# Second-layer conditioning formed by VectorE inside the first MLP, weight sums moved from GpSimd to VectorE, attentions in a new order: a two-layer hybrid diffusion step on one Trainium2 core

## The chip, the cores and the metric

The kernel runs on one core of a Trainium2 chip. The metric is device time in microseconds for one execution; runs are compared by their median. The core has a matrix engine (TensorE; PE in the profile, with the loads of its stationary operand shown as PEld), a vector engine (VectorE, DVE), a scalar engine (ScalarE, ACT), GpSimd (POOL) and SyncE (SP), which here issues every DMA. Matrices live in on-chip SBUF; TensorE writes into PSUM, of which there are eight banks, and VectorE and ScalarE read from there.

## The reference, cut to what matters

Two trunk layers (`DEPTH = 2`) run over 128 context tokens and 512 latent tokens, 640 in all, 1024 wide, in float32. Each layer is modulated by six vectors that come from one conditioning vector per token group:

```python
sh1, sc1, g1, sh2, sc2, g2 = jnp.split(jax.nn.silu(cvec) @ lw['w_ada'] + lw['b_ada'], 6, axis=-1)
h = rmsnorm(x, lw['norm1_g']) * (1 + sc1) + sh1
...
x = x + g1 * (mix @ lw['w_out'])
h2 = rmsnorm(x, lw['norm2_g']) * (1 + sc2) + sh2
x = x + g2 * (jnp.square(jax.nn.relu(h2 @ lw['w_up'])) @ lw['w_down'])
```

`w_ada` is 1024 x 6144 for each layer, and there are only two different vectors `cvec` (context and latent), so the conditioning of a layer is a product of a 1024 x 6144 matrix with two columns. Nothing in it depends on the tokens; it has to be there before the layer uses it: `sh1` and `sc1` (sections 0 and 1 below) at the layer's first normalisation, `g1` (section 2) at the output projection, sections 3, 4 and 5 in the MLP.

## The kernel before, in words

**Precision.** Every large product is formed from float32 values split into a rounded high part (type fp32r) and the rest: high x high, high x low, low x high. So a weight tile (`wr`, raw, 512 KB, 128 x 1024) is loaded by SP, copied into a high tile `wh` by ScalarE (L401 or L416), and the difference `wl` is formed by VectorE (L409, the helper `sub`). TensorE then does three matmuls for each piece.

**Stages.** After the input (to 48 us) each layer has a projection, the attentions, a second normalisation, and the MLP. Projection and attentions are planned by a list scheduler in the kernel's Python (class `Plan`): each piece of work is a task with an estimated cost, a priority and its operands, and the plan's order becomes the program's order for each engine. The order of the attention's parts is written by hand as a string of tokens (`"seq"` in `KP`, L64): `s0`, `s1` the windowed heads, `D0`, `d0`, `D1`, `d1` the differential heads with their preparation, `V0`, `M0`, `m0`, `M1`, `m1` the latent heads, `w0` to `w2` the output projections, and `c1` one conditioning of 256 columns.

**Conditioning before the change.** `conditioning` (L552) forms 256 columns of one section: two loads of 512 KB, sixteen matmuls of TensorE (L578, tile `pa`), a ScalarE copy, two transposes (L583), and two or three small VectorE operations that add the bias and, for sections 1 and 4, form the multiplier `amul`. Layer 0's first two sections are formed in the beginning, from wider loads. Its other sections, 2, 3, 4 and 5, and sections 1 and 0 of layer 1 are formed during layer 0's attentions (24 conditionings); sections 2, 4, 3 and 5 of layer 1 during layer 1's attentions (16).

**The MLP** isn't planned by `Plan` but written out as a loop (from L1745 on). The hidden width of 4096 is cut into eight groups of 512. A group's up-projection is two pairs of 128-wide tiles; each pair is done by seven products instead of eight (a Strassen-Winograd form over two halves of the model width and two halves of the tokens). The seven are called `A11 A12 S2 S3 S1 A22 S4`. One such product is a block: 12 matmuls of 320 columns (L1871). An up half of a group is therefore 14 blocks. A group's down-projection is eight blocks of 24 matmuls (L544 to L546). The order is: down 0, up 1, then up g+1 and down g in turn; down 7 is done in the next plan.

Seven products need sums. Those of the tokens are formed by VectorE during the first eight blocks (`wino_tokens`, tiles `Tl`, `Th`). Those of the weights are formed from the two raw tiles `r0` and `r1` of a pair by four GpSimd operations of 128 x 512: two early ones in `advance` (L1784) as soon as the second raw tile's load has been written into the program (`r1` low half, and `ws`), two late ones in `pool_late` (L1778) after the tile `A12` has been prepared (`r0` low half = S1's weights, `r0` high half = S4's).

Results: blocks A11, S2 and S1, S4 add into one PSUM bank X one after another, S3 and A22 into a bank Z, A12 into Y:

```python
z = {"A11": "X", "A12": "Y", "S2": "X", "S3": "Z", "S1": "X", "A22": "Z", "S4": "X"}[q]
new = q in ("A11", "A12", "S3")
```

After A11, S2 and S3 ScalarE copies the bank out (`pe`). After A12, S1 and A22 VectorE adds bank and copy (L1886) and squares the positive part (L1887); after S4 ScalarE takes the positive part (L1881) and VectorE squares it (L1882). One block later each result is split into the high and low part of `Gt` (ScalarE L401, VectorE L409). After a down block VectorE adds the product, times g2, to the residual `xT` (L747).

For each block the program's order is: its matmuls; the operations on its result; the split of the block before; two steps of the token sums; then `prep` (L1804), which prepares weight tiles. There are four `wh` and four `wl` buffers, so the tile prepared after a block is the one three tiles ahead, just when the block was the last user of a buffer. `prep` calls `advance`, which writes the loads into the program: four raw buffers, and the load of raw tile n is written once tile n-4 has been used. Each engine does its instructions in the program's order; SP issues a load when a raw buffer is free.

## Time and profile before

| | |
|---|---|
| runs | 1782.9, 1694.25, 1690.71 us (median 1694.25) |
| the profiled execution | 1687.62 us, of which the span from the first to the last instruction is 1685.8 us; mean granted TensorE clock 0.99 |

By stage, from the busy time by stretches:

| stretch, us | stage | us | PE busy | DVE busy | ACT busy | POOL busy |
|---|---|---|---|---|---|---|
| 0 to 48 | input, first conditioning | 48 | 32.05 | 30.28 | 23.53 | 0.20 |
| 48 to 160 | projection, layer 0 | 112 | 109.59 | 78.00 | 43.63 | 0.00 |
| 410 to 455 | second normalisation, first up-projection | 45 | 39.01 | 33.54 | 25.81 | 2.61 |
| 455 to 828 | MLP, layer 0 | 373 | 369.00 | 265.28 | 134.07 | 79.91 |
| 828 to 870 | last down-projection, normalisation | 42 | 41.33 | 34.06 | 22.18 | 0.00 |
| 870 to 984 | projection, layer 1 | 114 | 110.48 | 75.46 | 41.31 | 0.00 |
| 1228 to 1270 | second normalisation, first up-projection | 42 | 36.27 | 32.36 | 25.39 | 2.59 |
| 1270 to 1643 | MLP, layer 1 | 373 | 369.52 | 264.49 | 134.30 | 81.46 |
| 1643 to 1686 | last down-projection, output | 43 | 31.52 | 28.34 | 8.32 | 0.00 |

The attentions, 160 to 410 and 984 to 1228, are shown with the prediction.

How to read the profile's lines. A line of a stretch gives its bounds and length, then for each engine the busy microseconds and the number of instructions (x), the granted TensorE clock, the share of DMA in use and GB/s. A line of the timeline gives start, duration, engine, the line of the kernel, the operation, output <- inputs with shapes, and in brackets how long the engine stood idle before and what ended that. Durations overlap: an engine can begin an instruction a little before the last one has ended, so what one costs in a row of them is read from start to start. A line of waits gives who waited for whom, microseconds in total, how often, and the longest.

### The profile page before, as it was taken

What the parts mean: (1) busy time and instruction counts of PE and PEld (TensorE: products, weight loads), DVE (VectorE), ACT (ScalarE), POOL (GpSimd) and SP (SyncE); (2) the same over time, 40 slices, a digit from 0 to 9 for tenths busy, and PEclk for the clock granted to TensorE, in tenths of its full rate; (3) what the DMA queues carried; (4) which work ended last, traced back from release to release, by engine and by line L of the source; (5) the groups of instructions that cost most, each with busy time, mean ns of one, the idle gap of its engine ahead of it and who ended that gap; (6) DMA issues with size and microseconds to landing.
All of it is one profiled execution on the core that took longest, in us unless ns stands there. A gap on an engine that the chain in (4) does not pass through costs nothing.

```text
span 1685.8 us, 29293 instructions
## 1 busy us (share of the span) xinstructions
PE 1609.4 (95%) x11035; PEld 1443.1 (86%) x11035; DVE 1270.1 (75%) x3315; ACT 792.7 (47%) x1773; POOL 204.0 (12%) x164
## 2 busy tenths in 40 slices
PE   6999999898999999999999999999989999999997
PEld 4787678577999999999988766866889999999997
DVE  5875889877788666776586769999888866766666
ACT  4533776774544332333264346776463523343231
POOL 0000012000133122220000000300002322212200
PEclk9999999999999999999999999999999999999999
DMA  9433453532113212232223234124021212221121
GB/s 328 131 92 112 144 178 95 166 105 88 51 51 101 88 57 83 76 101 95 65 66 99 82 113 156 53 91 147 26 77 62 91 60 88 89 100 65 62 76 63
DMA packets 67388, 163.20 MB, mean 97 GB/s; under 512 B 6896, under 2 KB 31280, under 8 KB 67248
## 3 DMA queue, kind: packets, MB, share of 16 engines
q1 hardware_dynamic: 67248, 161.34, 29.5%
q8 instruction: 87, 1.43, 0.3%
q14 instruction: 53, 0.43, 0.1%
HBM read 153.15 MB, written 8.16 MB: 96 GB/s over the span
## 4 chain that ended last, share of the span: by engine, by line
PE 76%; DVE 14%; ACT 3%; DMA 2%; issue 2%; POOL 0%; DVEq 0%; SPq 0%; ACTq 0%; POOLq 0%
PE pu L1871 19%; PE pu L544 8%; PE pu L545 8%; PE pu L546 8%; PE po L544 3%; PE pt L1108 3%; PE O L1122 3%; PE po L546 3%; PE po L545 3%; PE pz L842 3%; PE pz L844 3%; PE pz L843 3%; DVE wl L409 2%; PE pu L1484 2%; PE pa L578 1%
## 5 line engine op out<-in xcount | busy, mean ns | idle before, releaser
L409 DVE TENSOR_TENSOR wl<-wr,wh 128x512 fp32r<-128x512 f32 (+2 forms) x290 | 289.3, 1018 | 68.0 <-ACT wh L401 34.2
L401 ACT ACTIVATE wh<-wr 128x512 fp32r<-128x512 f32 (+1 forms) x228 | 161.0, 736 | 272.1 <-PE pu L545 154.4
L544 PE MATMUL pu<-Gt,wh 128*128 128x384 f32 (+1 forms) x896 | 276.6, 309 | 1.2 <-DVE r L1469 1.2
L546 PE MATMUL pu<-Gt,wl 128*128 128x384 f32 (+1 forms) x896 | 276.5, 309 | 0.0
L545 PE MATMUL pu<-Gt,wh 128*128 128x384 f32 (+1 forms) x896 | 276.5, 309 | 0.0
L747 DVE SCALAR_TENSOR_TENSOR xT<-pu,ada,xT 128x128 f32<-128x128 f32 x336 | 133.0, 432 | 122.0 <-PE pu L546 121.7
L544 PEld LDWEIGHTS pu<-Gt,wh 128*128 128x128 f32 x896 | 169.8, 190 | 1.6 <-DVE r L1469 1.6
L545 PEld LDWEIGHTS pu<-Gt,wh 128*128 128x128 f32 x896 | 169.9, 190 | 0.0
L546 PEld LDWEIGHTS pu<-Gt,wl 128*128 128x128 f32 x896 | 169.8, 189 | 0.0
L1871 PE MATMUL pu<-Tl,wh 128*128 128x320 f32 x448 | 138.1, 308 | 0.0
L1871 PE MATMUL pu<-Th,wl 128*128 128x320 f32 x448 | 138.1, 308 | 0.0
L1871 PE MATMUL pu<-Th,wh 128*128 128x320 f32 x448 | 138.1, 308 | 0.0
L842 PE MATMUL pz<-wh,hh 128*128 128x512 f32 (+1 forms) x320 | 127.0, 397 | 3.8 <-DVE m L775 1.1
L844 PE MATMUL pz<-wh,hl 128*128 128x512 f32 (+1 forms) x320 | 122.4, 382 | 0.1
L843 PE MATMUL pz<-wl,hh 128*128 128x512 f32 (+1 forms) x320 | 121.8, 381 | 0.6 <-DVE wl L409 0.6
L1060 DVE TENSOR_REDUCE stt<-sps 128x1 f32<-128x640 f32 (+2 forms) x160 | 116.4, 736 | 7.3 <-PE sps L1053 4.2
L1871 PE MATMUL pu<-hh,wh 128*128 128x320 f32 x336 | 104.9, 312 | 7.5 <-DVE r L1886 7.5
L1068 ACT ACTIVATE quad<-sps,stt 128x640 f32<-128x640 f32 (+2 forms) x128 | 91.2, 713 | 41.1 <-DVE stt L1060 40.4
L1871 PE MATMUL pu<-hh,wl 128*128 128x320 f32 x336 | 104.3, 311 | 0.0
L1871 PE MATMUL pu<-hl,wh 128*128 128x320 f32 x336 | 104.2, 310 | 0.0
L1447 POOL TENSOR_TENSOR xT<-xT,tm 128x256 f32<-128x256 f32 (+1 forms) x32 | 33.1, 1038 | 574.2 <-ACT tm L1443 570.0
L409 POOL TENSOR_TENSOR wr<-wr 128x512 f32<-128x512 f32 x28 | 40.3, 1441 | 467.6 <-DMA wr<-in_w_up 313.2
(311 smaller groups left out, 3884.8 us busy)
## 6 DMA issues: line engine op xcount, KB each, us to landing
wr<-in_w_ada SPq DMA_DIRECT2D x80, 512.0 KB, 4.1
wr<-in_w_up SPq DMA_DIRECT2D x64, 512.0 KB, 3.3
wr<-in_w_down SPq DMA_DIRECT2D x64, 512.0 KB, 3.5
wr<-in_w_in SPq DMA_DIRECT2D x24, 512.0 KB, 3.6
wr<-in_w_out SPq DMA_DIRECT2D x16, 512.0 KB, 3.8
wq<-in_w_ada SPq DMA_DIRECT2D x6, 1024.0 KB, 11.9
wr<-in_w_in SPq DMA_DIRECT2D x8, 416.0 KB, 3.6
xT<-in_xT SPq DMA_DIRECT2D x4, 640.0 KB, 6.6
```

The source lines that it names most:

```text
L401: S.activation(out=out, in_=in_, func=AF.Copy)
L409: eng.tensor_tensor(out=out, in0=a, in1=b, op=ALU.subtract)
L544: T.matmul(out=out, lhsT=w[0], rhs=a[0], start=first, stop=False)
L545: T.matmul(out=out, lhsT=w[0], rhs=a[1], start=False, stop=False)
L546: T.matmul(out=out, lhsT=w[1], rhs=a[0], start=False, stop=last)
L747: V.scalar_tensor_tensor(out=xT[:, m, a:b], in0=po[:, a - a0:b - a0], scalar=ada[l][:, sec, m, s:s + 1], in1=xT[:, m, a:b], op0=ALU.mult, ...
L842: T.matmul(out=out, lhsT=h_at(h, "h", k, tk), rhs=wh[:, x], start=(k == 0), stop=False)
L843: T.matmul(out=out, lhsT=h_at(h, "h", k, tk), rhs=wl[:, x], start=False, stop=False)
L844: T.matmul(out=out, lhsT=h_at(h, "l", k, tk), rhs=wh[:, x], start=False, stop=(k == KD - 1))
L1060: add("V", tV(we) - 0.01, lambda st=st, j=j, view=view: V.tensor_reduce(out=st.t[:, j:j + 1], in_=view(), axis=AX.X if kind == "sw" else A ...
L1068: S.activation(out=out, in_=view(), func=AF.Exp, bias=st.t[:, j:j + 1], accum_out=st.t[:, 4 + j:5 + j])
L1871: T.matmul(out=out, lhsT=w_[:, k], rhs=a_[:, k], start=new and k == 0 and y == 0, stop=k == 3 and y == 2, skip_group_check=True)
```

## The change

1. **Layer 1's first three sections are no longer formed in the attentions.** `conds` holds sections 2, 4, 3, 5 for layer 0 (16 conditionings) and 4, 3, 5 for layer 1 (12).
2. **They are formed in layer 0's MLP by VectorE.** The host lays out `w_ada` of layer 1, sections 0 to 2, transposed (`w_adt`): 24 tiles of 128 output columns x (2 x 512) inputs. The inputs go along the free axis, in two halves `kk`. A tile is loaded into a raw buffer right behind each of the 24 down weights of groups 1 to 6. Once for each `kk`, `cond_rows` lays the two conditioning vectors along the free axis and on all partitions: two VectorE copies of a broadcast column, then eight transposes on TensorE into two PSUM banks and two ScalarE copies back. Four jobs for each tile then multiply 512 columns by one of the two rows and sum them (`scalar_tensor_tensor` with `accum_out`). Jobs start two blocks after the tile's load was written into the program, at most two a block, between the block's result and `prep`. `cond_end` adds the halves and the bias and forms `amul`, after the last block.
3. **The weight sums are VectorE's**, formed where they are used: the early two just before the tile A12 is prepared, the late two just after S2 (`early_sums`, `late_sums`). `ws` has one buffer instead of two.
4. **The attentions have a new order** (`seq`), with 16 and 12 tokens' worth of conditionings, and a few other settings of the planner.

```diff
-         "s": 2, "t": 3, "o": 1, "z": 4, "T": 2, "ws": 2}
+         "s": 2, "t": 3, "o": 1, "z": 4, "T": 2, "ws": 1}
...
-    {"weights": ("A", "V"), "caches": ("AV", "V"), "keys": ("A", "V"), "da": ("AV", "V"), "out": ("AV", "V"), "scale": "AV",
-     "lead": 40, "prep": 1000000.0, "tr": 900000.0, "up": ("A", "V"), "up_prio": 3500000.0, "evict": 1000000.0,
+    {"weights": ("A", "V"), "caches": ("AV", "V"), "keys": ("AV", "V"), "da": ("AV", "V"), "out": ("A", "V"), "scale": "AV",
+     "lead": 30, "prep": 1000000.0, "tr": 900000.0, "up": ("A", "V"), "up_prio": 3500000.0, "evict": 999995.0,
      "resid": (4, 4, 8, 8), "half": 3.0,
-     "seq": "c1 c1 c1 c1 s0 s0 c1 c1 s0 c1 c1 c1 c1 s0 s1 c1 s1 D0 s1 s1 c1 w0 "
-            "c1 w1 c1 d0 c1 c1 V0 c1 c1 c1 D1 c1 d1 d0 c1 d1 M0 c1 m0 m0 c1 w2 "
-            "M1 m1 m1"},
+     "seq": "c1 c1 c1 s0 c1 c1 s0 c1 s0 c1 s0 c1 c1 c1 s1 c1 c1 w0 s1 D0 s1 s1 "
+            "c1 w1 c1 c1 d0 V0 D1 d1 d0 M0 d1 m0 m0 M1 c1 w2 m1 m1"},
...
-     "lead": 30, "prep": 1000000.0, "tr": 900000.0, "up": ("A", "V"), "up_prio": 3500000.0, "evict": 1000000.0,
+     "lead": 30, "prep": 950000.0, "tr": 950000.0, "up": ("A", "V"), "up_prio": 3500000.0, "evict": 1000000.0,
...
-     "seq": "c1 s0 s1 s1 c1 c1 c1 s1 s1 D0 c1 s0 c1 c1 c1 s0 w1 s0 w0 c1 c1 c1 "
-            "d0 V0 D1 d0 c1 c1 c1 c1 d1 M0 d1 m0 m0 M1 w2 m1 m1"},
+     "seq": "c1 s1 s0 c1 s1 s1 c1 s1 c1 s0 c1 c1 D0 s0 c1 w1 s0 w0 c1 c1 d0 d0 "
+            "V0 D1 c1 d1 c1 M0 d1 m0 m0 w2 M1 m1 m1"},
...
-            conds = [(l, 2)] + ([(l + 1, 1), (l + 1, 0)] if l + 1 < DEPTH else []) + [(l, x) for x in (4, 3, 5)]
+            conds = [(l, x) for x in ((2, 4, 3, 5) if l == 0 else (4, 3, 5))]
...
-            def pool_late(p):
+            def early_sums(p):
+                r0, r1 = p["r"]
+                sub(V, r1[:, lo_], r0[:, lo_], r1[:, lo_])
+                p["ws"] = psum["ws"].tile([P, 512], F32, tag="ws", name="ws", bufs=RINGS["ws"])
+                sub(V, p["ws"], r1[:, hi_], r1[:, lo_])
+
+            def late_sums(p):
                 r0 = p["r"][0]
-                G.tensor_tensor(out=r0[:, lo_], in0=p["ws"], in1=r0[:, lo_], op=ALU.add)
-                sub(G, r0[:, hi_], r0[:, hi_], p["ws"])
+                V.tensor_tensor(out=r0[:, lo_], in0=p["ws"], in1=r0[:, lo_], op=ALU.add)
+                sub(V, r0[:, hi_], r0[:, hi_], p["ws"])
...
+                    elif kind == "c":
+                        dma(raw, i["w_adt"][b_, d_, a_])
+                        cond_q.append((at_block[0], (a_, b_, d_), cond_job(a_, b_, d_, raw)))
                     else:
                         dma(raw, i["w_up"][l, a_ + b_])
                         p = pair.setdefault(a_, {"r": []})
                         p["r"].append(raw)
-                        if b_:
-                            r0, r1 = p["r"]
-                            sub(G, r1[:, lo_], r0[:, lo_], r1[:, lo_])
-                            p["ws"] = psum["ws"].tile([P, 512], F32, tag="ws", name="ws", bufs=RINGS["ws"])
-                            sub(G, p["ws"], r1[:, hi_], r1[:, lo_])
...
+                cond = [(kk, sec, f) for kk in range(2) for sec in (1, 0, 2) for f in range(4)]
+                at_ = [n_ for n_, r in enumerate(raws_) if r[0] == "d" and 1 <= r[1] <= 6]
+                for n_, c in reversed(list(zip(at_, cond))):
+                    raws_.insert(n_ + 1, ["c", *c])
+
+            def cond_rows(kk, x):
+                if x == 0:
+                    for s_ in range(2):
+                        V.tensor_copy(cb[:, s_].rearrange("p (k n) -> p k n", k=4),
+                                      sc[:, 4 * kk:4 * kk + 4, s_:s_ + 1].to_broadcast([P, 4, P]))
+                    return
+                for s_ in range(2):
+                    pb = bank()
+                    for k in range(4):
+                        T.transpose(pb[:, k * P:(k + 1) * P], cb[:, s_, k * P:(k + 1) * P], ident)
+                    copy(S, cb[:, s_], pb)
...
+                        V.scalar_tensor_tensor(out=junk, in0=raw[:, 512 * fi:512 * fi + 512], scalar=1.0, in1=cb[:, s_],
+                                               op0=ALU.mult, op1=ALU.mult, accum_out=part[:, kk, at_, s_:s_ + 1])
...
+            def cond_step(b_, n):
+                while n and cond_q and cond_q[0][0] + 2 <= b_:
+                    n -= 1
+                    cond_q[0][2].pop(0)()
+                    if not cond_q[0][2]:
+                        done[cond_q.pop(0)[1]] = True
...
+                at_block[0] = b_
+                cond_step(b_, 2)
+                advance()
                 while state["tile"] < len(tiles) and last_use[state["tile"] - RINGS["wh"]] <= b_:
                     prep()
```

## The prediction, written before the change was run

> **What bounds the kernel now.** I read the page first, then the busy time by stretches, then the timeline and the waits around the few places where TensorE stands still. The page's head:

> ```profile
> span 1685.8 us, 29293 instructions
> PE 1609.4 (95%) x11035; PEld 1443.1 (86%) x11035; DVE 1270.1 (75%) x3315; ACT 792.7 (47%) x1773; POOL 204.0 (12%) x164
> ```

> TensorE is the bound nearly everywhere, so an edit is worth what it does to TensorE's own work and to its holes. By stretches (busy us of PE, PEld, DVE, ACT, POOL; attention of layer 0, an up and a down half of one MLP group, attention of layer 1):

> ```profile
> 160.00:410.00 250.00, 239.15 (x1939) 180.10 (x1932) 209.88 (x593) 176.00 (x439) 17.83 (x24) 0.99 0.43 136
> 563.70:588.30 24.60, 24.60 (x171) 24.60 (x170) 18.48 (x31) 12.60 (x25) 3.35 (x3) 1.00 0.34 110
> 588.30:616.40 28.10, 28.10 (x194) 28.10 (x193) 17.80 (x34) 5.70 (x11) 8.46 (x6) 1.00 0.16 55
> 984.00:1228.00 244.00, 231.47 (x1792) 176.79 (x1791) 218.45 (x603) 158.13 (x407) 19.36 (x24) 0.99 0.32 101
> ```

> In an MLP group TensorE has no hole at all, and VectorE is idle for 6.1 us of the up half and 10.3 us of the down half. In the attentions TensorE has holes of 10.9 and 12.5 us and VectorE is busy 84% and 90%.

> How closely TensorE hangs on VectorE inside an up half shows at the start of the MLP, where it does stand still (PE busy in the two holes, then the timeline before the first, then the whole kernel's waits of this kind):

> ```profile
> 490.90:494.20 3.30, 0.06 (x2) 0.05 (x1) 1.54 (x3) 0.63 (x1) 2.25 (x2) 0.91 0.00 0
> 1308.10:1311.20 3.10, 0.14 (x2) 0.06 (x1) 1.55 (x3) 0.63 (x1) 2.04 (x2) 1.00 0.00 0
> ...
> 486.84 0.49 DVE L409 TENSOR_TENSOR Gt<-r,Gt 128x320 fp32r<-128x320 f32 x1
> 487.69 1.30 POOL L409 TENSOR_TENSOR wr<-wr 128x512 f32<-128x512 f32 x1 [18.82 <-DMA wr<-in_w_up]
> 490.67 1.25 POOL L1781 TENSOR_TENSOR wr<-ws,wr 128x512 f32<-128x512 f32 x1
> 491.96 0.63 ACT L401 ACTIVATE wh<-wr 128x512 fp32r<-128x512 f32 x1 [3.57 <-POOL wr L1781]
> 492.62 1.07 DVE L409 TENSOR_TENSOR wl<-wr,wh 128x512 fp32r<-128x512 f32 x1 [3.08 <-ACT wh L401]
> 493.62 0.48 DVE L1886 TENSOR_TENSOR r<-pu,pe 128x320 f32<-128x320 f32 x1
> ...
> PE pu L1871 <- DVE r L1886: 7.5, 4, 3.2
> ```

> GpSimd's queue had the sums of the next pair ahead of the late sums of this one, and those waited for a load. ScalarE, VectorE and then TensorE waited behind it. The last link is the one that matters below: the matmuls of S4 add into the bank that S1 filled, so they wait until VectorE has read S1's result (L1886) out of it. TensorE went on as soon as that read was over. Between S1 and S4 lies one block. VectorE may therefore be about one block late in an up half, no more; a long queue of weight tiles prepared ahead doesn't help.

> **The change, part by part.**

> *Twelve conditionings leave the attentions* (8 of 24 in layer 0, 4 of 16 in layer 1). On the chain, sixteen such matmuls in a row, and eight transposes in a row, take:

> ```profile
> 211.22 1.07 PE pa L578 x16
> 165.87 0.88 PE pt L1108 x8
> ```

> A conditioning is 16 matmuls and 2 transposes: 1.07 + 2 x 0.11 = 1.3 us, so 10.4 us of TensorE in layer 0 and 5.2 in layer 1. With each go two 512 KB loads on SP's queue, a ScalarE copy and two or three small VectorE operations. These matmuls wait for nobody, so they also filled holes, and VectorE's share rises as the stage shrinks; the stages also get a new order whose effect no row shows. I count three quarters: -12 us. Bounds: -2 (they only filled holes) and -21 (all 15.6, and 5 of the 23 us of holes closed by the new order).

> *The weight sums go from GpSimd to VectorE*, four subtractions or additions of 128x512 a pair, 14 pairs a layer. Prices from the timeline of an up half; start to start, since one begins before the last has ended:

> ```profile
> 567.20 0.49 DVE L1886 TENSOR_TENSOR r<-pu,pe 128x320 f32<-128x320 f32 x1 [1.74 <-PE pu L1871]
> 567.72 0.49 DVE L1887 SCALAR_TENSOR_TENSOR r<-r 128x320 f32<-128x320 f32 x1
> 568.13 0.68 DVE L409 TENSOR_TENSOR wl<-wr,wh 128x512 fp32r<-128x512 f32 x1
> 568.73 0.69 DVE L409 TENSOR_TENSOR wl<-ws,wh 128x512 fp32r<-128x512 f32 x1
> ...
> 576.71 0.48 DVE L1882 SCALAR_TENSOR_TENSOR r<-pu,r 128x320 f32<-128x320 f32 x1
> 577.11 0.48 DVE L409 TENSOR_TENSOR Gt<-r,Gt 128x320 fp32r<-128x320 f32 x1
> ...
> 585.72 1.22 DVE L409 TENSOR_TENSOR wl<-wr,wh 128x1024 fp32r<-128x1024 f32 x1
> 586.86 0.48 DVE L1886 TENSOR_TENSOR r<-pu,pe 128x320 f32<-128x320 f32 x1
> ...
> 461.97 3.51 DVE L409 TENSOR_TENSOR wl<-wr,wh 128x512 fp32r<-128x512 f32 x2
> ```

> So a 512 costs 0.60, a 1024 1.14, reading a result and squaring it 0.93 (0.52 + 0.41), S4's single read 0.40, a 320 subtraction 0.40. A pair's sums are 2.4 us. In layer 1 that lifts an up half from 18.5 to 20.9 of 24.6 us: still covered, I take 0 (bounds -1 and +6, half a microsecond a pair, since all four come in one block). At the two starts the chain above goes: the late sums no longer stand behind the next pair's load. VectorE there has 4.8 us more to do for two pairs, 2.2 us of it paid by the two subtractions that took 3.51 us beside GpSimd instead of 1.2. The idle 3.08 us before 492.62 takes the rest, so of 3.2 and 3.0 us of hole about 2 us each is won: -4 (bounds -6 and 0).

> *The conditioning on VectorE.* 24 tiles of 512 KB, one behind each down weight of groups 1 to 6, each four multiply-and-sum jobs of 128x512. Their price isn't in the trace: no VectorE operation here writes out an accumulator. Below, it is 0.60 (same elements, two SBUF inputs, as L409). Above, the longest such row, 640 columns in 0.90, gives 0.72 for 512, and ScalarE's read-out of an accumulator adds 0.20: 0.92. The rows, with the chain's row of one up half and the page's row of a load:

> ```profile
> L1086 DVE SCALAR_TENSOR_TENSOR quad<-e,stt,quad 128x640 f32<-128x640 f32 x32 | 28.9, 902 | 0.0
> L1068 ACT ACTIVATION_READ_ACCUMULATOR quad<-sps,stt 128x1 f32 x128 | 25.5, 199 | 0.0
> ...
> 563.58 24.62 PE pu L1871 x168
> ...
> wr<-in_w_down SPq DMA_DIRECT2D x64, 512.0 KB, 3.5
> ```

> I take 0.70, nearer the plain row. [...]

> Now follow one up half. Its 14 blocks (A11 A12 S2 S3 S1 A22 S4, twice) take 24.62/14 = 1.76 us each. A tile's jobs are emitted two a block from the second block after its load. Going through the loop, the load of each down weight and of the conditioning tile behind it waits for one of four buffers, and these come free one after another in the up half; so all 16 jobs of a group land in the up half, where VectorE has 6 us to spare, and none in the down half, where it has 10. From the end of the 2nd block (A12) to the start of the 14th (S4) TensorE has 11 blocks, 19.4 us. In that time VectorE must do, in order, all that is queued up to its read of the 12th block (S1):
> - results: 4 x 0.93 + 0.40 + 0.52 = 4.6; their subtractions 5 x 0.40 = 2.0; weights 6 x 0.60 + 2 x 1.14 = 5.9. Together 12.5, as now, and covered;
> - sums of one pair, 2.4;
> - 12 of the 16 jobs, 8.4;
> - waits for loads. A tile's load starts when VectorE's subtraction frees a buffer and takes 3.5 us; about 2.5 us of VectorE's work stand between that and the job. About 1 us for two of the three tiles: 2.1 (bounds 0 and 4). Behind the waiting job stand the results that TensorE waits for.

> Sum 25.4, 6.0 us more than 19.4. The rest of the jobs slips into the down half and is covered there (17.8 of 28.1 now). Six groups: +36 us. Bounds: 0.60 and no waits gives 22.1, 2.7 a group, +16; 0.92 and 4 us gives 29.9, 10.5 a group, +63.

> *Forming the rows.* Twice, VectorE copies broadcast values right behind an A12 result, and TensorE must transpose them eight times before its next block. TensorE waits for 0.93 + 2 x 0.60 and some hop, 2.3, and transposes for 0.9: 3.2 each, +6.5 (bounds +2, transposes alone, and +10). The three closing operations come when the last jobs are long done, under eight down blocks: 0.

> Sum: -12 - 4 + 36 + 6.5 = +26.5. The profiled execution took 1687.6 us, its span of 1685.8 and 1.8 around it; that gives 1714. The fastest of the runs shown stands 3 us above the profiled one (1690.7, median 1694.25), so I forecast **1717 us** for the runs.

> **Rivals.**
> - *VectorE keeps up (the other side).* If 12 jobs and their waits fit into the 4.5 us that are left in the eleven blocks (19.4 - 12.5 - 2.4), the up halves cost nothing, and the sum is -9.5: 1681. It decides from 0.37 us a job without any wait. For it: the product itself is thrown away in a narrow type, so a faster pace isn't excluded. Against: every two-input row above runs at about one column in a nanosecond. Chance 0.12.
> - *The jobs run at half pace.* If reading back the sum takes a turn for each column, a job costs what 1024 columns cost, 1.14: 12 x 0.44 = 5.3 us more a group, +32, 1749. Against: L1887, two inputs in SBUF, runs no slower than L1886, but it sums nothing. [...] Chance 0.12.
> - *The attentions give nothing.* VectorE, at 84% and 90%, and the holes set their length: -2 instead of -12, 1727. For it the 12.5 us of holes in layer 1; against, 95% of PE in both. Chance 0.15.
> - *The forecast*, VectorE as the bound of six up halves: 0.57. The remaining 0.04: the new order closes most holes.

> **The numbers.** What a measurement of this kernel can tell from no change is about 2%, 34 us: 1660 and 1728. The forecast's own range, 1700 to 1735, lies on both sides of the upper bound, one quarter above it; the rival at half pace lies wholly above, the attentions' nearly half. Slower by over 2%: 0.57 x 0.25 + 0.12 + 0.15 x 0.45 = 0.33. Faster by over 2%: 0.03. Within: 0.64. The range reaches from VectorE nearly keeping up, with the attentions' full gain, to half pace: 1686 to 1748.

> **What would show it.** Right: TensorE busy less than its full time in the up halves of layer 0's groups 1 to 6, some 6 us a group, the waits named as L1871 behind L1886's read; VectorE above 95% there, with waits for conditioning tiles among its own; both halves of layer 1's groups still full; POOL without work in the MLPs; the holes near 491 and 1308 us smaller; attention stages 8 and 4 us shorter. Wrong: TensorE full in those up halves, or layer 1's MLP slower as well (then the sums, not the conditioning, are the load), or an attention that grew.

## The result and the profile after

The kernel after takes 1736.74 us (median of four runs, 1733.33 to 1737.38) against 1690.71 us before (median of 1682.73, 1690.71 and 1694.25). The ratio is 1.0274, with a 95% interval of 1.0255 to 1.0293: slower by 2.7%. A fourth run of the kernel before, 1782.9 us, was a slow one and is left out here. The forecast was 1717 us, with 1686 to 1748 as its range. The profiled execution took 1736.38 us, where the sum of the prediction gave 1714. The page's head (lines after the change that lie behind the removed ones are shifted: L1871 is now L1941, L1886 and L1887 are L1956 and L1957, L409 is L408):

```profile
span 1734.6 us, 28954 instructions
## 1 busy us (share of the span) xinstructions
PE 1616.4 (93%) x10835; PEld 1452.8 (84%) x10835; DVE 1348.2 (78%) x3600; ACT 787.1 (45%) x1763; POOL 35.1 (2%) x52
```

TensorE does 200 matmuls less than before and still shows more busy time: some of it ran slower. To see where, I cut both traces at the same four landmarks (first score matmul of an attention, first and last down-projection matmul of an MLP loop). Busy time by stretches, before: attentions and second norm of layer 0, MLP of layer 0, then the same of layer 1.

```profile
158.39:452.07 293.68, 276.84 (x2168) 215.76 (x2168) 242.47 (x682) 199.24 (x489) 18.56 (x25) 0.98 0.39 124
452.07:827.04 374.97, 370.97 (x2520) 370.44 (x2520) 267.25 (x464) 136.11 (x247) 81.79 (x56) 1.00 0.25 82
983.73:1269.24 285.51, 267.25 (x2024) 210.37 (x2024) 250.33 (x686) 182.98 (x462) 21.31 (x26) 0.98 0.31 98
1269.24:1642.53 373.29, 369.81 (x2520) 369.28 (x2521) 265.14 (x462) 134.79 (x244) 82.09 (x55) 1.00 0.23 77
```

After, the same four, then one up half and the down half behind it (layer 0), a stretch within that up half, and an up half of layer 1:

```profile
158.92:442.87 283.95, 266.21 (x2024) 211.94 (x2024) 239.23 (x660) 196.15 (x483) 17.60 (x24) 0.97 0.30 98
442.87:874.21 431.34, 390.33 (x2537) 383.64 (x2536) 337.64 (x716) 138.06 (x251) 0.00 (x0) 0.96 0.31 100
1031.08:1318.24 287.16, 262.88 (x1952) 210.27 (x1952) 250.53 (x679) 180.11 (x457) 17.29 (x24) 0.97 0.26 82
1318.24:1690.33 372.09, 371.94 (x2519) 369.37 (x2520) 274.45 (x518) 133.98 (x244) 0.00 (x0) 1.00 0.23 77
560.60:594.26 33.66, 27.00 (x169) 25.95 (x169) 26.81 (x58) 12.56 (x24) 0.00 (x0) 0.95 0.38 124
594.26:622.44 28.18, 28.18 (x195) 28.18 (x194) 20.70 (x47) 5.80 (x10) 0.00 (x0) 1.00 0.22 77
590.61:594.02 3.41, 2.94 (x11) 2.94 (x12) 1.96 (x6) 0.47 (x1) 0.00 (x0) 0.50 0.82 269
1425.00:1449.97 24.97, 24.97 (x170) 24.65 (x170) 19.92 (x35) 12.68 (x24) 0.00 (x0) 1.00 0.33 107
```

The loss is one stage: layer 0's MLP, 374.97 to 431.34 us, +56.4. Against it stand -9.7 in layer 0's attentions, +1.7 in layer 1's, -1.2 in layer 1's MLP, and +1.6 in all the rest: 48.8, the difference of the spans. Inside that MLP the down half is full (28.18 of 28.18) and the up half isn't: TensorE idles for 6.66 us of it, close to the forecast (6.0). But one column shows something that the prediction didn't have: PEclk, the granted clock, is 0.95 over the up half, and 0.50 in the 3.41 us from 590.61 on.

The timeline around that spot, where L1882 are the conditioning jobs and L1956 is VectorE's read of a result:

```profile
564.38 0.49 DVE L1956 TENSOR_TENSOR r<-pu,pe 128x320 f32<-128x320 f32 x1 [1.75 <-PE pu L1941]
...
580.42 0.69 DVE L1882 SCALAR_TENSOR_TENSOR junk<-wr,cb 128x512 bf16<-128x512 f32 x1 [0.92 <-DMA wr<-in_w_adt]
...
586.70 0.69 DVE L1882 SCALAR_TENSOR_TENSOR junk<-wr,cb 128x512 bf16<-128x512 f32 x1 [1.03 <-DMA wr<-in_w_adt]
...
587.46 0.31 PE L1941 MATMUL pu<-Th,wl 128*128 128x320 f32 x1
...
589.19 0.69 DVE L1882 SCALAR_TENSOR_TENSOR junk<-wr,cb 128x512 bf16<-128x512 f32 x1
589.80 0.08 DVE L1882 DVE_READ_ACCUMULATOR junk<-wr,cb 128x1 f32 x1
589.92 0.69 DVE L1882 SCALAR_TENSOR_TENSOR junk<-wr,cb 128x512 bf16<-128x512 f32 x1
590.54 0.08 DVE L1882 DVE_READ_ACCUMULATOR junk<-wr,cb 128x1 f32 x1
590.54 0.48 DVE L1956 TENSOR_TENSOR r<-pu,pe 128x320 f32<-128x320 f32 x1
...
591.08 0.63 PE L1941 MATMUL pu<-hh,wh 128*128 128x320 f32 x1 [3.30 <-DVE r L1956]
```

Read it from the bottom. S4's first matmul stood for 3.30 us until VectorE had read S1's result out of the bank. VectorE, in its own order, had two jobs and a weight tile ahead of that read, and further up it had stood twice, for about 1 us each, with a job in hand whose tile hadn't landed. From the read of A12's result (564.38) to S4 (591.08) went 26.7 us; the prediction had put together 25.4, with 19.4 for TensorE alone. And the matmul that ends the wait takes 0.63 us where the one before it took 0.31.

The waits of that kind in the whole kernel (who waits <- for whom, us, times, longest), and the jobs among the groups by form:

```profile
PE pu L1941 <- DVE r L1956: 26.5, 11, 3.4
DVE junk L1882 <- DMA wr<-in_w_adt: 21.2, 22, 1.5
```

```profile
L1882 DVE SCALAR_TENSOR_TENSOR junk<-wr,cb 128x512 bf16<-128x512 f32 x96 | 66.2, 690 | 22.9 <-DMA wr<-in_w_adt 21.2
L1882 DVE DVE_READ_ACCUMULATOR junk<-wr,cb 128x1 f32 x96 | 7.9, 82 | 0.0
```

### The profile page after: what moved, and what is told of

Its sections match the earlier page's. It is cut to its first block, busy times and chain, and to the rows that moved or that the text cites. A ratio compares the mean times of both kernels' runs of the same rounds, so it can differ in the third digit from the quotient of the medians.

```text
span 1734.6 us, 28954 instructions
## 1 busy us (share of the span) xinstructions
PE 1616.4 (93%) x10835; PEld 1452.8 (84%) x10835; DVE 1348.2 (78%) x3600; ACT 787.1 (45%) x1763; POOL 35.1 (2%) x52
## 4 chain that ended last, share of the span: by engine, by line
PE 67%; DVE 20%; DMA 4%; ACT 4%; issue 3%; DVEq 0%; SPq 0%; ACTq 0%
PE pu L1941 11%; PE pu L543 7%; PE pu L544 7%; PE pu L545 7%; DVE wl L408 4%; DMA wr<-in_w_adt 3%; PE pt L1107 3%; PE po L543 3%; PE O L1121 3%; PE po L544 3%; PE po L545 3%; PE pz L841 3%; PE pz L843 2%; PE pz L842 2%; PE pu L1483 2%
## 5 line engine op out<-in xcount | busy, mean ns | idle before, releaser
L408 DVE TENSOR_TENSOR wl<-wr,wh 128x512 fp32r<-128x512 f32 (+2 forms) x290 | 256.7, 903 | 47.0 <-ACT wh L415 33.9
L543 PEld LDWEIGHTS pu<-Gt,wh 128*128 128x128 f32 x896 | 171.8, 192 | 1.6 <-DVE r L1468 1.6
L544 PEld LDWEIGHTS pu<-Gt,wh 128*128 128x128 f32 x896 | 171.6, 191 | 0.0
L1941 PE MATMUL pu<-Th,wh 128*128 128x320 f32 x448 | 141.2, 315 | 11.5 <-ACT pe L400 11.4
L1941 PE MATMUL pu<-Tl,wh 128*128 128x320 f32 x448 | 138.8, 310 | 0.0
L1941 PE MATMUL pu<-Th,wl 128*128 128x320 f32 x448 | 138.7, 310 | 0.0
L1941 PE MATMUL pu<-hh,wh 128*128 128x320 f32 x336 | 109.2, 325 | 26.6 <-DVE r L1956 26.5
L400 ACT ACTIVATE Gt<-r 128x320 fp32r<-128x320 f32 (+2 forms) x128 | 59.4, 467 | 106.3 <-DVE r L1957 97.2
L1941 PE MATMUL pu<-hh,wl 128*128 128x320 f32 x336 | 107.1, 319 | 0.0
L1941 PE MATMUL pu<-hl,wh 128*128 128x320 f32 x336 | 107.0, 319 | 0.0
L1941 PEld LDWEIGHTS pu<-Th,wh 128*128 128x128 f32 x448 | 84.6, 189 | 16.2 <-ACT pe L400 16.0
## 6 DMA issues: line engine op xcount, KB each, us to landing
wr<-in_w_up SPq DMA_DIRECT2D x64, 512.0 KB, 3.4
wr<-in_w_down SPq DMA_DIRECT2D x64, 512.0 KB, 3.5
wr<-in_w_ada SPq DMA_DIRECT2D x56, 512.0 KB, 4.0
wr<-in_w_in SPq DMA_DIRECT2D x24, 512.0 KB, 3.6
wr<-in_w_adt SPq DMA_DIRECT2D x24, 512.0 KB, 3.6
wr<-in_w_out SPq DMA_DIRECT2D x16, 512.0 KB, 4.4
```

Of the source, the lines that this page charges most:

```text
L400: S.activation(out=out, in_=in_, func=AF.Copy)
L408: eng.tensor_tensor(out=out, in0=a, in1=b, op=ALU.subtract)
L543: T.matmul(out=out, lhsT=w[0], rhs=a[0], start=first, stop=False)
L544: T.matmul(out=out, lhsT=w[0], rhs=a[1], start=False, stop=False)
L1941: T.matmul(out=out, lhsT=w_[:, k], rhs=a_[:, k], start=new and k == 0 and y == 0, stop=k == 3 and y == 2, skip_group_check=True)
```

## The experiments

The theory: twelve jobs and their waits for loads stand, in VectorE's order, ahead of the result that S4 waits for; TensorE's hole is the first loss, and the half clock behind the hole the second. Rivals: the weight sums are the load; the loads themselves are; the jobs cost too much wherever they stand; the attentions' order. Each set of runs has its own runs of the kernel before, so ratios are compared, and differences between sets are given by the ratios, at 1690 us for the kernel before. Some expectations rest on "the account of the loop": the loop's program order followed with the profile's durations; it isn't shown here.

**1. The sums alone** (on the kernel before: `early_sums` and `late_sums` as in the change, nothing else).

```diff
-                            sub(G, r1[:, lo_], r0[:, lo_], r1[:, lo_])
...
+                sub(V, r1[:, lo_], r0[:, lo_], r1[:, lo_])
```

> The kernel before with one part of the change alone: the weight sums on VectorE, formed where they are used; conditioning and attentions as before. My theory (VectorE has room for the sums, the holes at the two starts shrink): both MLPs' up halves stay at 24.6 to 24.9 us with TensorE full, each start 2 us shorter, 1688 us against 1692. Rival (the sums, 2.4 us a pair on VectorE, are what holds TensorE up): some 3 us more in each of 14 up halves, 1735 us.

Measured: 1685.83 us, 0.9966 of before (0.9951 to 0.9982). Layer 0's MLP and one of its up halves:

```profile
449.99:822.79 372.80, 371.85 (x2521) 369.23 (x2520) 275.51 (x520) 135.35 (x247) 0.00 (x0) 1.00 0.25 82
557.46:582.41 24.95, 24.95 (x170) 24.62 (x169) 19.92 (x35) 12.70 (x24) 0.00 (x0) 1.00 0.34 107
```

Alone, the sums cost next to nothing: the up half is full, though it takes 0.33 us longer (24.95 instead of 24.62). The two MLPs get 2.2 and 1.2 us shorter in this trace: 3.9 and 2.9 us are won in the first two up halves, where the holes are gone, and 1.7 lost in the other five. VectorE is busy only 8.3 us more over this MLP (275.51 instead of 267.25) for 34 us of sums, since its own operations get shorter without GpSimd's beside them (the subtraction of 128x512 from 839 to 687 ns, mean of 170). The rival of the sums alone falls. No run has the jobs in the MLP with the sums left on GpSimd.

**2. The change without the conditioning in the MLP.**

```diff
-                for n_, c in reversed(list(zip(at_, cond))):
-                    raws_.insert(n_ + 1, ["c", *c])
+                V.memset(part, 0.0)
```

> The kernel after without the 24 conditioning tiles, the rows and the jobs in the MLP; the partial sums are set to zero, so sections 0 to 2 of layer 1 hold their bias alone (that part of the computation is left out). My theory (all of the loss lies in the jobs, the loads they wait for and what TensorE's holes bring with them): layer 0's MLP takes 372 us as layer 1's does, 1680 us, 57 below the kernel after. Rival (attention order or sums are the load): 1715 us or more.

Measured: 1676.68 us, 0.9920 (0.9893 to 0.9947). Its layer 0 MLP is experiment 1's again:

```profile
442.48:815.29 372.81, 371.85 (x2520) 369.25 (x2520) 275.54 (x521) 135.36 (x247) 0.00 (x0) 1.00 0.25 82
```

So jobs, rows and loads cost 431.34 - 372.81 = 58.5 us, and the two lines of these MLPs split them: TensorE's idle time grows from 0.96 to 41.01 (+40.1), its busy time from 371.85 to 390.33 (+18.5).

**3 and 4. The same jobs later**: four, then six blocks after the load was written, not two.

```diff
-                while n and cond_q and cond_q[0][0] + 2 <= b_:
+                while n and cond_q and cond_q[0][0] + 6 <= b_:
```

> The kernel after, but a tile's jobs may begin four blocks after its load was written into the program, not two. By the account of the loop from the profile's durations the waits for conditioning tiles vanish (18 us in all), and part of the jobs moves into the down halves: 24 us off the holes, and perhaps half of the half-clock windows (15 us now) go with them: 1707 us. Rival (VectorE's work in the MLP as such, or the conditioning's loads, take the time wherever they fall): 1735 us. Rival (the waits for loads are all of it): holes gone, 1690 us.

> The kernel after with a lag of six blocks. The account gives 39 us off the holes, since most jobs now fall into the down halves where VectorE has 10 us to spare, and then the half-clock windows after the holes should go too (up to 15 us): 1685 us, a little below the kernel before. If the half-clock windows are no consequence of the holes, 1698 us. Rival (the jobs' work as such): 1735 us.

Measured: 1697.98 us, 1.0046 (1.0028 to 1.0064), with four; 1682.67 us, 0.9960 (0.9942 to 0.9979), with six. Waits for tiles are gone with both. With four, TensorE still waits for results, but not for long:

```profile
PE pu L1941 <- DVE r L1956: 12.1, 10, 1.5
```

and the expectation was 9 us too high. TensorE's idle time fell by 22 us (24 expected), but its busy time by 14: not half but all of the half clock in this MLP went (PEclk 1.00, longest hole left 2.35 us). With six: the MLP, an up half, a down half.

```profile
442.66:822.65 379.99, 374.90 (x2536) 370.96 (x2536) 333.78 (x716) 139.38 (x251) 0.00 (x0) 1.00 0.35 113
553.26:578.47 25.21, 25.21 (x169) 24.64 (x169) 21.86 (x44) 12.81 (x24) 0.00 (x0) 1.00 0.39 124
578.47:606.62 28.15, 28.15 (x195) 28.15 (x194) 25.00 (x61) 5.80 (x10) 0.00 (x0) 1.00 0.35 114
```

The same 96 jobs, the same 24 loads, the same engine: now most of them are in the down half, where VectorE's busy time rises to 25.00 of 28.15 us and nobody waits. One number in the program is worth about 53 us (51.4 in this MLP). The jobs as such were never too much; the rivals of the jobs' price and of the loads fall. What is left over experiment 2 is 7.2 us, 5.9 of it in the two up halves with rows (54.32 instead of 51.21, 28.03 instead of 25.20 us).

**5. The hole filled.** TensorE gets something to do while it waits, in the kernel after.

```diff
+                    if cond and q == "S4" and f % 4:
+                        pf = bank()
+                        for k in range(16):
+                            T.matmul(out=pf[:, 0:320].rearrange("p (t n) -> p t n", n=64),
+                                     lhsT=wh[:, 128 * (k % 4):128 * (k % 4) + 128], rhs=operand("A22")[0][:, k % 4],
+                                     start=k == 0, stop=k == 15, skip_group_check=True)
                     bh, bl = operand(q)
```

> The kernel after with sixteen extra matmuls of 320 columns (2.35 us, their result is read by nobody) ahead of the last S4 of every up half of layer 0, where TensorE stands still for 3.3 us anyway. Theory (the half-clock windows are a consequence of the long hole): with TensorE busy for 2.35 of those 3.3 us the holes shrink to about 1 us, the clock stays full behind them, and the run gets shorter by up to 12 of the 15 us that the windows cost, although TensorE does more work: 1725 us. Rival (the windows come from the mix of the stage, not from the hole): 1737 us as after. Rival (the extra matmuls delay S4 themselves): above 1740 us.

Measured: 1724.74 us, 1.0206 (1.0184 to 1.0227), 12 us below the kernel after (11.5 by the ratios, 9.4 in the MLP of the two traces) with 16.5 us more work for TensorE. Its MLP and the up half from the timeline above:

```profile
443.92:865.91 421.99, 394.11 (x2648) 387.41 (x2648) 336.86 (x716) 137.94 (x251) 0.00 (x0) 1.00 0.32 102
561.89:594.27 32.38, 28.05 (x185) 27.00 (x185) 25.50 (x55) 12.56 (x24) 0.00 (x0) 1.00 0.38 119
```

```profile
589.16 2.51 PE L1940 MATMUL pu<-Th,wh 128*128 128x320 f32 x16
592.41 0.41 PE L1947 MATMUL pu<-hh,wh 128*128 128x320 f32 x1 [0.74 <-DVE r L1962]
```

Jobs, loads and VectorE's lateness are as they were, and PEclk is 1.00 over this MLP (0.96 in the kernel after) and over the up half (0.95). So the half clock came from the hole, and it is a loss of its own.

**6. The loads alone**: tiles loaded and held in their buffers as in the change, each job empty.

```diff
-                if (sec, f) == (1, 0):
-                    jobs += [lambda x=x: cond_rows(kk, x) for x in range(2)]
+                if raw is not None:
+                    return [lambda: None] * 4
```

> The kernel after with the 24 tiles loaded at the same places and held in their buffers for the same blocks, but without the jobs and the rows; partial sums set to zero (sections 0 to 2 of layer 1 hold their bias alone, that part of the computation is left out). Theory (the loads cost only where VectorE waits for them with a job in hand): as without the tiles at all, 1677 us, all up halves at 25.0 us. Rival (12.6 MB more in layer 0's MLP, or raw buffers held, delay the other weights): 1690 us or more.

Measured: 1675.82 us, 0.9922 (0.9902 to 0.9943), and an MLP of 372.81 us, experiment 2's to the hundredth. 12.6 MB more cost nothing unless VectorE comes to them too early.

**7. The two steps of a row apart** (lag of six).

```diff
-                    jobs += [lambda x=x: cond_rows(kk, x) for x in range(2)]
+                    nop = [lambda: None]
+                    jobs += [lambda: cond_rows(kk, 0)] + 3 * nop + [lambda: cond_rows(kk, 1)] + 3 * nop
```

> The lag of six blocks, with the two steps of a row apart: the transposes are written two blocks behind VectorE's copies, and the first job two blocks behind the transposes. Theory (each of the two up halves with rows is 3 us longer since TensorE waits 2.1 us for the copies, and only 0.9 us is its own work): 4 us less than with the lag alone, 1679 us. Rival (the transposes and the copy back cost the 3 us wherever they stand): 1683 us.

Measured: 1679.65 us, 0.9946 (0.9926 to 0.9966); the MLP takes 377.24 us instead of 379.99. With the steps together TensorE stood for 2.1 and 2.0 us until the copies were done; apart it doesn't stand, and a row costs 1.7 and 1.5 us instead of 3.1 and 2.8.

**8 and 10. The order of layer 1's attentions.** The old order without the four conditionings that left, and the new order with four put back (both with the lag of six):

```diff
-     "seq": "c1 s1 s0 c1 s1 s1 c1 s1 c1 s0 c1 c1 D0 s0 c1 w1 s0 w0 c1 c1 d0 d0 "
-            "V0 D1 c1 d1 c1 M0 d1 m0 m0 w2 M1 m1 m1"},
+     "seq": "c1 s0 s1 s1 c1 c1 c1 s1 s1 D0 c1 s0 c1 c1 c1 s0 w1 s0 w0 c1 c1 c1 "
+            "d0 V0 D1 d0 d1 M0 d1 m0 m0 M1 w2 m1 m1"},
```

```diff
-            conds = [(l, x) for x in ((2, 4, 3, 5) if l == 0 else (4, 3, 5))]
+            conds = [(l, x) for x in (2, 4, 3, 5)]
...
-            "V0 D1 c1 d1 c1 M0 d1 m0 m0 w2 M1 m1 m1"},
+            "V0 D1 c1 c1 c1 c1 c1 d1 c1 M0 d1 m0 m0 w2 M1 m1 m1"},
```

> The lag of six blocks, with layer 1's attentions in the order and with the settings of before, less the four conditionings that went to the MLP. The attentions to the end of the first up-projection of layer 1 took 285.5 us before, 284.9 with the sums alone, and 284 to 288 in the kernels with the new order. If the new order eats what the four conditionings give: 281 us there, 1679 us in all. If the four conditionings only filled holes (they are worth nothing): 284 to 285 us there, 1683 us in all. If the old order depends on them: above 288.

> The lag of six blocks with section 2 of layer 1 formed a second time, in layer 1's attentions as before: the new order with four more conditionings, the missing fourth of old and new order with 16 and 12 (old 16: 284.9 us, new 12: 284.4, old 12: 298.3, attentions to the first down-projection). If a conditioning costs its 1.3 us of TensorE in the new order: 290 us there, 1688 in all. If conditionings fill holes in this order too: 284 to 286, 1683 in all. If, as the old order did, the order hangs on its number of conditionings: above 293.

Measured: 1692.64 us, 1.0026 (1.0015 to 1.0037), and 1695.04 us, 1.0043 (1.0026 to 1.0060), where the lag alone has 0.9960. The stage, from the busy time by stretches of four kernels: the sums alone (old order, 16), the lag of six (new, 12), experiment 8 (old, 12), experiment 10 (new, 16).

```profile
979.60:1264.49 284.89, 265.98 (x2024) 208.71 (x2024) 250.23 (x686) 183.10 (x462) 18.92 (x24) 0.99 0.32 98
```

```profile
979.44:1263.83 284.39, 261.54 (x1951) 209.06 (x1951) 250.16 (x679) 180.18 (x457) 17.13 (x24) 0.98 0.27 83
```

```profile
981.32:1279.58 298.26, 268.94 (x1951) 210.31 (x1951) 250.90 (x681) 180.02 (x454) 18.88 (x24) 0.97 0.25 79
```

```profile
986.18:1283.12 296.94, 270.47 (x2023) 212.16 (x2023) 253.42 (x691) 180.74 (x457) 17.20 (x24) 0.97 0.30 94
```

Each order is good with its own number of conditionings and 12 to 14 us worse with the other's. From 16 to 12, each with its order, VectorE's busy time stays at 250.2 and the stage's length with it, while TensorE is busy 4.4 us less. That fits conditionings that filled time which was there anyway, but doesn't show it by itself, since the order changed with their number. Taking work out of a hand-made order can lengthen it. Which of the order's tokens does it was not tried, nor another place for the four that were put back in one row.

**9. Half as much in each job** (lag of two, as in the kernel after).

```diff
-                        V.scalar_tensor_tensor(out=junk, in0=raw[:, 512 * fi:512 * fi + 512], scalar=1.0, in1=cb[:, s_],
+                        V.scalar_tensor_tensor(out=junk[:, 0:256], in0=raw[:, 512 * fi:512 * fi + 256], scalar=1.0, in1=cb[:, s_, 0:256],
```

> The kernel after (lag of two) with jobs over 256 of their 512 columns, so sections 0 to 2 of layer 1 miss half of their inputs (that part of the computation is left out). Loads, rows and the number of instructions are the same. Theory (VectorE's time in the eleven blocks sets the hole before S4): a job costs about 0.43 us, and the account of the loop gives 18 us less in holes although the waits for loads grow from 18 to 25 us, and with the holes most of the half-clock windows go (9 us by the run with the filled hole): 1710 us. Rival (the waits for loads, or the number of instructions, set it): 1730 us or more.

Measured: 1712.96 us, 1.0141 (1.0126 to 1.0156). Waits for tiles grow while TensorE's shrink, as the account has it:

```profile
PE pu L1941 <- DVE r L1956: 17.3, 12, 2.4
DVE junk L1882 <- DMA wr<-in_w_adt: 29.6, 22, 2.7
```

The holes before the second S4 of an up half are 2.2 to 2.4 us long now, and a stretch of half clock still follows three of the six.

Halving the jobs' price gives about 22 us; placing them right (experiment 4) gives 53 at the full price.

**11. One job a block** instead of two, with the lag of six and the rows' steps apart.

```diff
-                cond_step(b_, 2)
+                cond_step(b_, 1)
```

> The lag of six blocks, the two steps of a row apart, and one job a block instead of two: the jobs are spread still more evenly over up and down halves. Theory: the last 0.25 us an up half and part of what the rows still cost (1.5 to 1.7 us each) go, 1 to 3 us less than with two a block: 1677 to 1679 us, where the kernel without any conditioning in the MLP takes 1676 to 1677. Rival (spreading no longer matters): 1680 us. Rival (tiles stay longer in their buffers and weights come late): 1690 us or more.

Measured: 1678.44 us, 0.9938 (0.9925 to 0.9952); against experiment 7 that is not to be told apart, but the trace shows the step. The MLP and an up half:

```profile
445.36:819.94 374.58, 373.62 (x2537) 371.04 (x2536) 333.79 (x716) 137.89 (x251) 0.00 (x0) 1.00 0.36 115
553.71:578.68 24.97, 24.97 (x170) 24.65 (x169) 22.11 (x44) 12.68 (x24) 0.00 (x0) 1.00 0.42 136
```

The conditioning costs 1.8 us more than none at all, and the whole is faster than the kernel before by 0.6%.

## Why the prediction came out as it did

The direction and the main mechanism were right: VectorE, late in its own order, holds up TensorE in six up halves. The sum fell short by 22 us of the profiled execution, and the time lies 2 us above the forecast's own range (1700 to 1735). That the wide range holds it is in part luck: its upper end was put there for jobs at half pace, which didn't come, and a loss that wasn't in the sum took their place. No change beyond 2% had been given 0.64, slower by over 2% only 0.33. By the prediction's own steps:

- *Up halves, +36.* The size is right, the path only in part. TensorE's idle time in layer 0's MLP grew by 40.1 us over the same kernel without jobs; 3.1 of it are the two waits for the rows, so 37. In the half shown here twelve jobs lay ahead of S4's release, start to start 0.73 and 0.62 us (0.70 taken), and VectorE's waits for tiles came to 2.1 us (2.1 taken). But the hole before the last S4 is 3.2 to 3.4 us, not 6.0; the six are 20 of the 37. Another 6.6 are the same wait before the S4 of a half's first pair, and 10.5 come through a link that the prediction didn't have: TensorE waits for ScalarE's copy of a bank (`pe`). In the half shown, and then in the whole kernel:

```profile
568.39 0.63 ACT L400 ACTIVATE wh<-ws 128x512 fp32r<-128x512 f32 x1 [3.54 <-DVE ws L408]
568.93 0.42 ACT L400 ACTIVATE pe<-pu 128x320 f32<-128x320 f32 x1
569.40 0.41 PE L1941 MATMUL pu<-Th,wh 128*128 128x320 f32 x1 [1.61 <-ACT pe L400]
...
PE pu L1941 <- ACT pe L400: 11.4, 11, 1.8
```

ScalarE had stood 3.54 us for `ws`, a weight sum that VectorE forms since the change, here behind two jobs; the copy that TensorE needs stood behind it in ScalarE's order. Without jobs this kind of wait is 0.9 us in the whole MLP (experiment 2). So jobs and sums on one engine meet here; how much of the loss needs both is open. A side remark failed too: VectorE was to be above 95% busy there and is at 80% (26.81 of 33.66). It isn't short of time over the half; it is late in its order.
- *Rows, +6.5.* Right: 3.1 us of waits and 3.1 of TensorE's work (374.90 - 371.85 in experiment 4), 6.1.
- *The half clock, not in the sum at all.* TensorE's busy time there grew by 18.5 us; less the rows' 3.1, 15.4 are left. The stretches at PEclk 0.50 in this MLP, five of 3.41 and two of 6.83 us, are 30.7 us, half of which is 15.4. This is the larger part of what the sum lacked. The prediction counted a hole as its length; but behind each of the six holes of 3.2 to 3.4 us came such a stretch, and a seventh behind a hole of 1.8 us. Before the change only one lies in this MLP, at the end of the hole near 491 us: the prediction had quoted that very row, with its PEclk of 0.91, and read only the busy time in it. That the clock went back to 1.00 with the holes filled (experiment 5) makes the hole the cause. Its length alone doesn't decide, as the last section shows. Of the 3.41 us ahead of each of the seven, TensorE's matmuls filled 4% to 48%.
- *Attentions, -12.* -8.1 in all, 3.9 short. Layer 0 gave 9.7, with about 8 counted, so the share of three quarters was fair there; no run parts the new order's share in it. Layer 1 lost 1.7, with 4 counted as gain. An attention that grew was one of the prediction's signs of being wrong, but 1.7 us lie within what one and the same order shows (the kernels here with that order take 284.4 to 290.2 us for the stage, 285.5 and 284.9 with the old one). No gain there fits the rival that these matmuls only filled holes.
- *MLP starts, -4, and layer 1's sums, 0.* The sums alone give 2.2 and 1.2 us in their trace, so the net is right, but by two misses that nearly cancel: the starts gave 6.8, more than the bound of 6, and the sums cost 0.33 us in each of five later up halves a layer, 3.3 in all, where 0 was counted.

15.4 + 3.9 are 19 of the 22 us; of the rest 1.6 lie in the stages between, which the sum left alone, 1 in the up halves and 0.6 in the starts and sums. Of the rivals, VectorE at half pace would have come nearest to this time, for another reason: its job of 1.14 us isn't in the trace. There a job of 128x512 takes 690 ns, about what the weight subtraction of that shape takes (686 ns), and reading out its accumulator is a second instruction, 82 ns long.

## What to carry to other kernels

Work that is handed to an engine with spare time has to be placed where that time is: look at the engine's idle time by stage, and at what stands behind the new work in the engine's own order, not at its share of the span. Price a hole of TensorE by its length and by the clock that follows it; where a hole that can't be avoided halves the clock, filling it with work nobody needs can be cheaper (experiment 5: 12 us less than the kernel after, with 16.5 us more work). An order that was fitted by hand belongs to its amount of work, and has to be fitted again when work is taken out.

## What the runs showed of the hardware

That extra matmuls made the program 9 to 12 us faster had not been expected before the trace of the kernel after was read: 112 of them, 16.5 us of TensorE's time, kept PEclk at 1.00 through an MLP where it had been 0.96.

```profile
587.20:590.61 3.41, 0.57 (x4) 0.31 (x3) 3.34 (x10) 0.00 (x0) 0.00 (x0) 1.00 0.44 125
628.16:631.57 3.41, 1.63 (x12) 1.36 (x11) 3.25 (x8) 1.17 (x3) 0.00 (x0) 1.00 0.00 0
508.61:512.02 3.41, 1.91 (x15) 1.95 (x16) 1.65 (x5) 1.44 (x4) 0.00 (x0) 1.00 0.01 2
510.90:514.31 3.41, 1.29 (x11) 1.06 (x10) 3.02 (x8) 0.47 (x1) 0.00 (x0) 1.00 0.00 0
514.31:517.72 3.41, 3.41 (x16) 3.41 (x14) 1.25 (x2) 2.23 (x4) 0.00 (x0) 0.50 0.01 2
```

Experiments 4 and 10 run the same MLP with the same two holes, of 2.1 and 2.0 us. In 4 each lies across two steps and the clock stays full; in 10 each empties most of one step, and the two up halves with rows take 1.5 us longer each (55.83 instead of 54.32 for the first two together, 29.56 instead of 28.03). So in these two traces what a hole of about 2 us cost hung on where the steps lay; experiment 3's two longest holes, 2.3 us each, also lay across two steps, and the clock stayed full.

VectorE's subtraction of 128x512 is shorter without GpSimd's sums beside it, in the kernel before and in experiment 1:

```profile
L409 DVE TENSOR_TENSOR wl<-wr,wh 128x512 fp32r<-128x512 f32 x170 | 137.0, 839 | 16.5 <-ACT wh L401 16.5
L409 DVE TENSOR_TENSOR wl<-wr,wh 128x512 fp32r<-128x512 f32 x170 | 112.1, 687 | 0.3 <-ACT wh L401 0.2
```

The subtractions of 128x1024 and 128x320 in layer 0's MLP went from 1351 to 1224 and from 586 to 486 ns, while the addition that reads a PSUM bank (L1886) takes 487 ns in both. That is why 34 us of sums raised VectorE's busy time there by only 8.3 us.
